# A chunked recurrence between dense products: two groups of small products per chunk and a third chunk in flight

## The chip, the cores and the metric

The kernel runs on one core of one Trainium2 chip. The time is the device time of one execution, in microseconds (us). The engines are PE (TensorE: matmuls, with its weight loads shown apart as PEld), DVE (VectorE), ACT (ScalarE), POOL (GpSimd) and SP (SyncE, which here only issues DMAs). Each engine works through its own list of instructions in order; semaphores hold an instruction back until what it needs is there.

## The reference, cut to what matters

The kernel computes one layer of a hybrid backbone for 1152 tokens (1024 latent, 128 context) of width 1024: a half-step feed-forward block, a mixer (latent attention beside a gated recurrence that runs in both directions over the tokens), and a second half-step feed-forward block. The change touches the recurrence alone. Per head (8 heads, key and value width 64) and direction, the reference is:

```
def hgrn2_chunked(q, k, logf, v, s0):
    ...
    b = jnp.cumsum(logf.reshape(B, n, CHUNK, H, DK), axis=2)
    diff = b[:, :, :, None] - b[:, :, None, :]
    decay = jnp.where(mask, jnp.exp(jnp.where(mask, diff, 0.0)), 0.0)
    A = jnp.einsum('bntshk,bnthk,bnshk->bnhts', decay, qc, kc)
    o_intra = jnp.einsum('bnhts,bnshv->bnthv', A, vc)
    dS = jnp.einsum('bnshk,bnshv->bnhkv', kc * jnp.exp(g[:, :, None] - b), vc)
    def step(S, inp):
        gj, dSj = inp
        return jnp.exp(gj)[..., None] * S + dSj, S
    ...
    o_inter = jnp.einsum('bnthk,bnhkv->bnthv', qc * jnp.exp(b), S_prev)
```

So for each block of tokens three things are wanted: the masked matrix A of decayed products of queries and keys, the state's increment dS, and the chain of states S, from which the outputs are A times V plus queries times S.

## The kernel before, in words

**Stages.** `run` does the first feed-forward block, then the mixer, then the second block. The mixer begins with `hgrn`, which holds both the recurrence and the large projections of the mixer's input. The projections are what keeps PE busy there: each is a dense product over 384 tokens, 24 matmuls (`mm3`, lines 551 to 553, written to a bank called `mm`), cut in two halves of 12. The recurrence consists of very small products, and they are put between halves of dense ones.

**Chunks.** The tokens are cut in three chunks of 384 (three blocks of 128), and the eight heads are taken one after another, so there are 24 chunks. Both directions of a head lie in the two halves of the 128 partitions. Per chunk:

- `scan_pre` (no matmuls) makes from the gates the scaled keys and queries of blocks of 8 tokens: Kb, Qb, and KE, QP, which carry the decay to the edge of the block. It is cut in five steps.
- `scan_lev` climbs the levels. Level 0 multiplies Kb with Qb in blocks (24 matmuls, two banks, one for each direction). The levels m = 8, 16, 32 and 64 each multiply a half-filled copy of the keys, `kr[m]`, with QP (12, 12, 12 and 6 matmuls, one bank). After a level's product DVE and POOL scale QP (line 1135), and DVE scales KE, by the decays of the neighbouring block; ACT makes the next `kr` from KE (`key_half`). So the product of a level needs QP as scaled after the level before it. Results are taken out of the banks by DVE under a mask (lines 1105, 1140) or by ACT (line 1124). Then KE is transposed (`kt`, line 1150), copied by ACT, and multiplied with V (`dS`, line 1160), which ACT copies out (line 1161).
- After the third chunk of a head, `scan_out` runs the chain of states on DVE (line 1170, 14 steps), multiplies A and S with V and QP (`po`, lines 1180 and 1183), and ACT copies the outputs. When four of these are done for a pair of heads, ACT squares the outputs (line 820), PE takes their means (`ops`, line 1194) and DVE and ACT normalise (`rstd`).

**Order.** A generator stands for each piece of work. For p = 0, 1, ... the loop in `hgrn` takes `cur` (the chunk p) and `old` (the chunk before) and alternates between `group(...)`, which takes one step of each generator named, and `slots(k)`, which takes k halves of dense products, with a step of `scan_pre` for the next chunk in each. There are three groups and 3, 2 or 3, and 2 slots per chunk. A scheduler then orders each engine's list by the order of the program and by when it expects operands, and it may move an instruction of DVE or ACT by some places.

**Banks.** Of the eight PSUM banks three are a ring for the levels (`lv`), two for the dense products (`mm`), and three for the rest (`sm`: kt, dS, po, the transposes of V called vt, and ops). A product that takes the next bank of a ring waits until what stood there has been read.

Of the kernel before, what the change touches and what calls it, by code (L numbers as in the profile page):

```python
# [9 lines left out]
F32 = mybir.dt.float32  # L10
# [9 lines left out]
P = 128  # L20
# [7 lines left out]
NCH = T // CW  # L28
# [5 lines left out]
H = 8  # L34
# [59 lines left out]
class Trunk:  # L94
# [783 lines left out]
    def hgrn(self):  # L878
# [76 lines left out]
            pass  # L955
        self.group()
        work = chain.from_iterable(map(work_of, range(H)))
        old = cur = out = last = None
        for p in range(H * NCH + 1):
            h, n = divmod(p, NCH)  # L960
            old, cur, pre = cur, None, iter(())
            if h < H:
                cur = self.scan_lev(d, ORDER[n])
            if p + 1 < H * NCH:
                h1, n1 = divmod(p + 1, NCH)
                while min(heads[h1].get("nf", 0), pairs[h1 // 2].get("nq", 0)) <= n1:
                    next(work)
                if n1 == 0:
                    last, d = d, scan_of(h1)
                pre = self.scan_pre(d, ORDER[n1])  # L970

            def slots(k):
                for _ in range(k):
                    next(work, None)
                    next(pre, None)
                    self.tick()

            self.group(old, cur)
            slots(3)
            self.group(old, cur, old, out)  # L980
            slots(2 + p % 2)
            self.group(cur, out, old)
            out = None
            if p and n == 0:
                out = self.scan_out(last if h < H else d)
                next(out)
            slots(2)
            for _ in pre:
                pass
        self.group(out, out)  # L990
        todo = list(range(KT // 2))
        for i, _ in enumerate(work):
            self.tick()
# [30 lines left out]
    def scan_pre(self, d, b):  # L1024
        nc = self.nc
        fs, q, QP, hh = d["f"], d["pair"]["q"], d["QP"], d["h"] % 2
        A, B = slice(0, 64), slice(64, P)
        c0 = b * CW
        X, Y = self.XY
        tmp = self.tmp  # L1030
        fv = fs[:, c0 : c0 + CW].rearrange("p (n e) -> p n e", e=8)
        kk = tmp("kk")
        nc.scalar.activation(kk[A], fs[A, c0 : c0 + CW], AF.Copy, scale=-1.0, bias=1.0)
        nc.scalar.activation(kk[B], fs[B, c0 + 1 : c0 + CW + 1], AF.Copy, scale=-1.0, bias=1.0)
        qx = tmp("qx")
        for r in (A, B):
            nc.scalar.copy(qx[r], q[64 * hh : 64 * hh + 64, c0 : c0 + CW])
        yield
        for out, pos, off, eng in ((X, (2, 1, 0), 1, nc.vector), (Y, (4, 5, 6, 7), 0, nc.gpsimd)):
            for n, o in enumerate(pos):  # L1040
                ov, iv = out[:, :, o : o + 1], fv[:, :, o + off : o + off + 1]
                if n == 0:
                    nc.scalar.copy(ov, iv)
                else:
                    eng.tensor_mul(ov, iv, out[:, :, pos[n - 1] : pos[n - 1] + 1])
        nc.vector.reciprocal(Y[:, :, 0:3], X[:, :, 0:3])
        yield
        nc.vector.reciprocal(X[:, :, 4:8], Y[:, :, 4:8])
        yield
        Kb, Qb, KE = tmp("Kb", 2), tmp("Qb", 2), tmp("KE", 3)  # L1050
        flat = lambda t: t.rearrange("p n e -> p (n e)")
        for r, x, y in ((A, X, Y), (B, Y, X)):
            nc.vector.tensor_mul(Kb[r], kk[r], flat(x)[r])
            nc.vector.tensor_mul(Qb[r], qx[r], flat(y)[r])
        yield
        TK, TQ, Tm = tmp("TK", 3, (P, 48)), tmp("TQ", 3, (P, 48)), tmp("T8", 3, (P, 48))
        f8 = fs[:, c0 + 8 : c0 + 8 + CW - 7 : 8]
        nc.vector.tensor_copy(TK[A], Y[A, :, 7])
        nc.vector.tensor_copy(TK[B], X[B, :, 0])
        nc.vector.tensor_mul(TQ[A], X[A, :, 0], fv[A, :, 0])  # L1060
        nc.vector.tensor_mul(TQ[B], Y[B, :, 7], f8[B])
        nc.vector.tensor_mul(Tm, TK, TQ)
        e8 = lambda t: t.rearrange("p (n e) -> p n e", e=8)
        bc = lambda t, m: t.unsqueeze(2).to_broadcast([t.shape[0], t.shape[1], m])
        qp = QP[:, c0 : c0 + CW]
        nc.vector.tensor_tensor(e8(KE), e8(Kb), bc(TK, 8), ALU.mult)
        nc.gpsimd.tensor_tensor(e8(qp), e8(Qb), bc(TQ, 8), ALU.mult)
        d["pre"] = Kb, Qb, KE, Tm
        yield

    def scan_lev(self, d, b):
        nc = self.nc
# [31 lines left out]
        for dst, mi, (_, ps) in zip((A1, A2), (0, 1), pair):  # L1104
            nc.vector.copy_predicated(dst, mb(mi), ps[:, :, :G])
        hm = lambda t, m: t.rearrange("p (n h m) -> p n h m", h=2, m=m)

        def key_half(m):
            kr = self.kr[m]
            nc.scalar.copy(hm(kr, m)[A, :, 0], hm(KE, m)[A, :, 0])  # L1110
            nc.scalar.copy(hm(kr, m)[B, :, 1], hm(KE, m)[B, :, 1])

        key_half(8)
        yield
        for li, m in enumerate((8, 16, 32, 64)):
            ps = lv()
            blocks = diag
            if m >= G:
                blocks = [(slice(u, u + m), slice(u + m, u + 2 * m)) for u in range(0, P, 2 * m)]
# [15 lines left out]
                eng.tensor_tensor(v, v, bc(tt[r], m), ALU.mult)  # L1135
            nc.vector.tensor_mul(Tn, tL, tR)
            if m < 64:
                key_half(2 * m)
            if m < G:
                nc.vector.copy_predicated(A1, mb(2 + li), ps[:, :, :G])  # L1140
            if m == 16:
# [1338 lines left out]
```

## Time and profile before

| | us |
|---|---|
| median of three runs | 2806.74 (2804.63 to 2808.57) |
| the profiled execution, its own time | 2808.74 |
| its span, first to last instruction | 2806.9 |
| PE busy, all of the span | 2755.8 (98%) |
| DVE busy, all of the span | 2044.2 (73%) |
| the recurrence: first level-0 product to last `ops` | 865 to 1388 |

The profile's rows give a start and a length in us, the engine, the line, the operation and the names as "written<-read", and in square brackets how long the engine stood idle before and what released it. A matmul's record is longer than the time until the next one starts, since they overlap: what counts on PE is the distance from start to start, some 0.17 to 0.18 us for a dense matmul here. A 32-wide or 64-wide product is shown as two records. The granted clock of PE was 1.00 of full speed all through the recurrence.

### The profile page before, as it was taken

How to read it: one execution, taken by the hardware profiler on the slowest of the kernel's cores; microseconds unless marked ns; L12 is line 12 of the kernel's file. 1: busy time of each engine (PE TensorE's matmuls, PEld its weight loads, DVE VectorE, ACT ScalarE, POOL GpSimd, SP SyncE). 2: the span in 40 equal slices, each digit the busy share in tenths (PEclk: the TensorE clock that was granted, in tenths of full speed). 3: DMA queues.
4: the chain of work that ended last, by engine and by line, in shares of the span. 5: the costliest groups of instructions: out<-in, count | busy, mean ns of one | idle time of the engine just before them, and what ended most of it. 6: DMA issues, size and time to landing. Idle time of an engine off the chain costs nothing. (4 is left out here: it accounts for less than half of the span.)

```text
span 2806.9 us, 55765 instructions
## 1 busy us (share of the span) xinstructions
PE 2755.8 (98%) x21248; PEld 2631.0 (94%) x21248; DVE 2044.2 (73%) x4461; ACT 1301.1 (46%) x2695; POOL 928.1 (33%) x983
## 2 busy tenths in 40 slices
PE   8999999999999999999999999999999999999998
PEld 8999999999999998899998788689999999999997
DVE  8877777677778888888456777867666765568875
ACT  6532323322166677666436777741642222334332
POOL 0133323454221222222233444431414343433451
PEclk9999999999999999999999999999999999999999
DMA  6733333653121111212512000273453444357521
GB/s 259 231 129 120 125 126 125 241 202 111 58 94 59 44 61 41 66 48 81 189 64 98 19 15 28 86 246 119 141 176 130 161 136 140 111 175 244 160 85 68
DMA packets 219579, 337.66 MB, mean 120 GB/s; under 512 B 23664, under 2 KB 141360, under 8 KB 219312
## 3 DMA queue, kind: packets, MB, share of 16 engines
q1 hardware_dynamic: 218880, 333.96, 35.5%
q8 instruction: 168, 2.75, 0.4%
q14 instruction: 99, 0.81, 0.1%
q10 hardware_dynamic: 432, 0.14, 0.0%
HBM read 248.47 MB, written 85.54 MB: 119 GB/s over the span
## 5 line engine op out<-in xcount | busy, mean ns | idle before, releaser
L1932 PE MATMUL b<-xo,wo 128*128 128x288 f32 x3552 | 483.7, 295 | 0.9 <-DVE wo L1907 0.9
L1932 PEld LDWEIGHTS b<-xo,wo 128*128 128x128 f32 x3552 | 475.4, 188 | 1.2 <-DVE wo L1907 1.2
L1932 PE MATMUL b<-bh,wo 128*128 128x288 f32 x1776 | 365.9, 295 | 0.0
L551 PE MATMUL mm<-xh,wh 128*128 128x384 f32 x928 | 322.9, 348 | 4.5 <-DVE sg L863 3.1
L553 PE MATMUL mm<-xh,wl 128*128 128x384 f32 x928 | 313.3, 338 | 0.0
L552 PE MATMUL mm<-xl,wh 128*128 128x384 f32 x928 | 312.5, 337 | 0.0
L1932 PEld LDWEIGHTS b<-bh,wo 128*128 128x128 f32 x1776 | 288.8, 188 | 0.0
L581 DVE SCALAR_TENSOR_TENSOR x<-dn,modt,x 128x256 f32<-128x256 f32 (+4 forms) x472 | 225.7, 499 | 82.3 <-PE dn L553 81.2
L1932 PE MATMUL b<-bl,wo 128*128 128x288 f32 x888 | 261.8, 295 | 0.0
L1906 ACT CAST wo<-raw 128x512 fp32r<-128x512 f32 x185 | 114.7, 621 | 222.5 <-issue 91.3
L2133 PE MATMUL d<-xd,wd 128*128 128x288 f32 x1344 | 181.5, 296 | 6.4 <-DVE x L2120 5.3
L2133 PEld LDWEIGHTS d<-xd,wd 128*128 128x128 f32 x1344 | 178.7, 188 | 9.1 <-issue 3.6
L1907 DVE TENSOR_TENSOR wo<-raw,wo 128x512 fp32r<-128x512 f32 x185 | 127.5, 690 | 80.4 <-ACT wo L1906 78.0
L551 PEld LDWEIGHTS mm<-xh,wh 128*128 128x128 f32 x928 | 174.2, 188 | 11.1 <-DVE sg L863 3.6
L552 PEld LDWEIGHTS mm<-xl,wh 128*128 128x128 f32 x928 | 174.4, 188 | 0.9
L553 PEld LDWEIGHTS mm<-xh,wl 128*128 128x128 f32 x928 | 174.5, 188 | 0.0
L1629 POOL TENSOR_TENSOR ehl<-e,ehl 128x512 fp32r<-128x512 f32 x93 | 124.1, 1339 | 151.3 <-ACT ehl L1627 80.4
L405 DVE SCALAR_TENSOR_TENSOR junk<-wada,cb 128x512 bf16<-128x512 f32 x224 | 164.7, 735 | 7.7 <-DMA wada<-in_w_aT 6.9
L1932 PEld LDWEIGHTS b<-bl,wo 128*128 128x128 f32 x888 | 167.4, 189 | 0.0
L1902 POOL TENSOR_TENSOR ws<-raw 128x256 f32<-128x256 f32 x74 | 69.8, 964 | 271.8 <-DMA raw<-in_w 242.9
L551 PE MATMUL ps<-bh,wh 128*128 128x288 f32 (+1 forms) x448 | 135.6, 303 | 1.4 <-DVE sl L1854 1.1
L1907 DVE TENSOR_TENSOR wo<-ws,wo 128x512 fp32r<-128x512 f32 x74 | 70.2, 948 | 86.4 <-ACT wo L1906 86.0
(478 smaller groups left out, 7172.5 us busy)
## 6 DMA issues: line engine op xcount, KB each, us to landing
raw<-in_w SPq DMA_DIRECT2D x148, 256.0 KB, 3.3
wada<-in_w_aT SPq DMA_DIRECT2D x112, 256.0 KB, 2.9
raw<-in_w SPq DMA_DIRECT2D x42, 512.0 KB, 3.9
raw<-in_w_in SPq DMA_DIRECT2D x41, 512.0 KB, 3.7
xr<-xd SPq DMA_DIRECT2D x56, 288.0 KB, 4.1
hr<-hs SPq DMA_DIRECT2D x26, 576.0 KB, 5.7
hb<-hd SPq DMA_DIRECT2D x44, 288.0 KB, 3.6
hs<-et SPq DMA_DIRECT2D x84, 144.0 KB, 2.2
```

The costliest lines, as they stand in the source:

```text
L405: nc.vector.scalar_tensor_tensor(junk, ws[n % 2], 1.0, cs[s], ALU.mult, ALU.mult, accum_out=o)
L551: pin(nc.tensor.matmul(ps, wh, xh, start=start and i == 0, stop=False))
L552: pin(nc.tensor.matmul(ps, wh, xl, start=False, stop=False))
L553: self.last_mm = nc.tensor.matmul(ps, wl, xh, start=False, stop=stop and i == n - 1)
L581: nc.vector.scalar_tensor_tensor(self.x[m][:, a:b], ps[:, a - lo : b - lo], self.modt[:, gm, m, s : s + 1], self.x[m][:, a:b], ALU.mult, A ...
L1629: eng.tensor_sub(el, e, eh)
L1902: nc.gpsimd.tensor_tensor(o[:, c], x[:, c], y[:, c], op)
L1906: nc.scalar.copy(wh, src[i])
L1907: nc.vector.tensor_sub(wl, src[i], wh)
L1932: nc.tensor.matmul(ps, w[:, k], x[:, k, :QW], start=first, stop=last, skip_group_check=home != i)
L2133: nc.tensor.matmul(ps, w[:, k], xv, start=start, stop=stop, skip_group_check=home != i)
```

## The change

The loop keeps three chunks in flight (`older`, `old`, `cur`) and has two groups per chunk, with 4 slots after the first and 3 or 4 after the second; it runs one round longer. Level 0 and the level of 8 are now one step of `scan_lev`; the `kr` for 8 is made at the end of `scan_pre`. The level of 8 takes its bank from the ring `sm` instead of `lv`. The chain of states begins after the first group of the second round of the next head, and both halves of the output products stand in the second group. No instruction is added or taken away on any engine.

```
-        old = cur = out = last = None
-        for p in range(H * NCH + 1):
+        older = old = cur = out = last = None
+        for p in range(H * NCH + 2):
             h, n = divmod(p, NCH)
-            old, cur, pre = cur, None, iter(())
+            older, old, cur, pre = old, cur, None, iter(())
...
-            self.group(old, cur)
-            slots(3)
-            self.group(old, cur, old, out)
-            slots(2 + p % 2)
-            self.group(cur, out, old)
+            self.group(older, old, cur)
             out = None
-            if p and n == 0:
+            if p > 1 and n == 1:
                 out = self.scan_out(last if h < H else d)
                 next(out)
-            slots(2)
+            slots(4)
+            self.group(out, old, cur, out, old)
+            slots(3 + p % 2)
             for _ in pre:
                 pass
-        self.group(out, out)
...
         nc.gpsimd.tensor_tensor(e8(qp), e8(Qb), bc(TQ, 8), ALU.mult)
+        self.key_half(KE, 8)
         d["pre"] = Kb, Qb, KE, Tm
         yield
+
+    def key_half(self, KE, m):
+        kr, src = [t.rearrange("p (n h m) -> p n h m", h=2, m=m) for t in (self.kr[m], KE)]
+        for r, side in ((slice(0, 64), 0), (slice(64, P), 1)):
+            self.nc.scalar.copy(kr[r, :, side], src[r, :, side])
...
-        key_half(8)
-        yield
         for li, m in enumerate((8, 16, 32, 64)):
-            ps = lv()
+            ps = self.pp.tile([P, 3, 64], F32, tag="sm", bufs=3, name="lv8") if m == 8 else lv()
...
             if m < 64:
-                key_half(2 * m)
+                self.key_half(KE, 2 * m)
```

How PE's list moves for one chunk, away from the ends of the recurrence. In these rows `kr_9121` is the `kr` of level 8, `kr_9122` of 16, `kr_9123` of 32 and `kr_9124` of 64, and "..." stands for halves of dense products (12 `mm` matmuls each). Before:

```order
L1098 MATMUL lv<-QP,kr_9123 32x32 x12
L1098 MATMUL lv<-Qb,Kb 32x32 x24
...
L1098 MATMUL lv<-QP,kr_9124 64x64 x6
L1098 MATMUL lv<-QP,kr_9121 32x32 x12
L1150 MATMUL kt<-ident,KE 128x128 x3
...
L1098 MATMUL lv<-QP,kr_9122 32x32 x12
L1160 MATMUL dS<-V,kT 64x64 x6
```

And now:

```order
L1155 MATMUL dS<-V,kT 64x64 x6
L1101 MATMUL lv<-QP,kr_9123 32x32 x12
L1101 MATMUL lv<-Qb,Kb 32x32 x24
L1101 MATMUL lv_10715<-QP,kr_9121 32x32 x12
...
L1101 MATMUL lv<-QP,kr_9124 64x64 x6
L1101 MATMUL lv<-QP,kr_9122 32x32 x12
L1145 MATMUL kt<-ident,KE 128x128 x3
```

The same 75 products of a chunk stand in two runs instead of three; dS is now that of the chunk two places back. Counted over the whole recurrence, from the first level-0 product to the last `ops`, PE's list has 77 runs of small products between dense ones before, and 54 in the change.

At the place where a pair's outputs are normalised (three times within the loop), PE's list before has

```order
L1098 MATMUL lv<-QP,kr_9122 32x32 x12
L1180 MATMUL po<-Af,V 64x128 x2
...
L1180 MATMUL po<-Af,V 64x128
L1160 MATMUL dS<-V,kT 64x64 x6
...
L1098 MATMUL lv<-QP,kr_9123 32x32 x12
L1098 MATMUL lv<-Qb,Kb 32x32 x24
L1194 MATMUL ops<-osq,onesb 128x384 x3
```

and now (`lv_11939` is the level of 8, in the ring `sm`)

```order
L1155 MATMUL dS<-V,kT 64x64 x6
L1101 MATMUL lv<-QP,kr_9123 32x32 x12
L1101 MATMUL lv<-Qb,Kb 32x32 x24
L1101 MATMUL lv_11939<-QP,kr_9121 32x32 x12
L1189 MATMUL ops<-osq,onesb 128x384 x3
```

Of the five tiles of the three-bank ring that this run fills, the second `ops` takes the bank of dS and the third takes that of the level of 8, both filled in the same run.

DVE's list after the first group, where a head's chain of states starts (the scaling of QP after level 32, the masked copies of level 0, the scaling after level 8, its masked copy, the chain, then KE for the next levels and the next chunk's Kb):

```order
L1130 TENSOR_TENSOR QP<-QP,T_10556 64x6x32
L1165 SCALAR_TENSOR_TENSOR S<-S,Gall,dS 64x64 x2
L1108 COPY_PREDICATED A_0_9127<-mask,lv 128x96
L1108 COPY_PREDICATED A_9129<-mask,lv 128x96
L1130 TENSOR_TENSOR QP<-QP,T_10600 64x24x8
L1135 COPY_PREDICATED A_0_9127<-mask,lv_10715 128x96
L1165 SCALAR_TENSOR_TENSOR S<-S,Gall,dS 64x64 x7
L1130 TENSOR_TENSOR KE<-KE,T_10875 64x6x32 x2
L1130 TENSOR_TENSOR KE<-KE,T_10923 64x24x8 x2
L1050 TENSOR_TENSOR Kb<-kk,X 64x384
```

The two scalings of QP stand next to their products; the chain follows at once. At the end of the recurrence PE's list had 24 dense matmuls between the last dS and the last outputs and 24 between these and the last `ops`; now it has 12 and 18.

More of the change, by code (lines that the diff above doesn't have):

```diff
@@ L1106, in scan_lev @@
         hm = lambda t, m: t.rearrange("p (n h m) -> p n h m", h=2, m=m)
[L1108 to L1111, printed above, removed]
-        key_half(8)
-        yield
         for li, m in enumerate((8, 16, 32, 64)):
-            ps = lv()
+            ps = self.pp.tile([P, 3, 64], F32, tag="sm", bufs=3, name="lv8") if m == 8 else lv()
             blocks = diag
```

## The prediction

> **What bounds the kernel now.** I read the page first, for the engine that is never free.
>
> ```profile
> PE 2755.8 (98%) x21248; PEld 2631.0 (94%) x21248; DVE 2044.2 (73%) x4461; ACT 1301.1 (46%) x2695; POOL 928.1 (33%) x983
> ```
>
> PE is, so whatever shortens PE's list or its waits in the recurrence shortens the kernel, as nothing else is near its limit over the span. Next the stretches: the recurrence whole, without its end, and its most crowded 80 us (columns: length, then busy time of PE, PEld, DVE, ACT, POOL, PE's clock, DMA).
>
> ```profile
> 865.00:1388.00 523.00, 511.26 (x6130) 477.86 (x6129) 405.59 (x1040) 348.31 (x862) 126.06 (x204) 1.00 0.22 73
> 865.00:1345.00 480.00, 468.26 (x5767) 437.58 (x5767) 391.90 (x1008) 327.29 (x821) 118.11 (x197) 1.00 0.18 60
> 1145.00:1225.00 80.00, 75.29 (x936) 69.77 (x935) 69.10 (x165) 53.62 (x133) 22.77 (x33) 1.00 0.16 50
> ```
>
> PE is idle for 523.0 - 511.3 = 11.7 us of the recurrence, at full clock. DVE is busy for 82% (391.9 of 480), in the worst stretch for 86%: not a bound, but an engine with a queue. Who PE waits for there (us in total, times, longest):
>
> ```profile
> PE lv L1098 <- DVE QP L1135: 7.0, 6, 1.8
> PE mm L551 <- DVE sg L863: 3.1, 2, 1.6
> PE lv L1098 <- DVE A L1105: 0.7, 1, 0.7
> PE lv L1098 <- POOL QP L1135: 0.3, 1, 0.3
> PE mm L551 <- DVE q L779: 0.3, 1, 0.3
> PE mm L551 <- ACT sg L751: 0.2, 1, 0.2
> ```
>
> So 8.0 us in 8 waits are level products that wait for the scaling of QP (or, once, for a bank); 3.6 us are dense products that wait for a bank of their own. Beside the waits there is a cost that counts as busy: the seam where PE goes from dense to small products and back. The timeline of PE around two runs, one of a level's product alone, one of dS alone:
>
> ```profile
> 1362.45 0.33 PE L552 MATMUL mm<-xl,wh 128*128 128x384 f32 x1
> 1362.62 0.34 PE L553 MATMUL mm<-xh,wl 128*128 128x384 f32 x1
> 1362.88 0.40 PE L1098 MATMUL lv<-QP,kr 128*32 128x32 f32 x24
> 1363.21 0.44 PE L551 MATMUL mm<-xh,wh 128*128 128x384 f32 x1
> 1363.49 0.34 PE L552 MATMUL mm<-xl,wh 128*128 128x384 f32 x1
> ...
> 1374.91 0.57 PE L1160 MATMUL dS<-V,kT 128*64 128x64 f32 x12
> 1375.41 0.44 PE L551 MATMUL mm<-xh,wh 128*128 128x384 f32 x1
> 1375.69 0.34 PE L552 MATMUL mm<-xl,wh 128*128 128x384 f32 x1
> ```
>
> Dense matmuls start 0.17 to 0.18 us apart (1362.45 to 1362.62). The last one before a run is followed after 0.26 us (1362.62 to 1362.88), the first one after it after 0.28 us (1363.21 to 1363.49, 1375.41 to 1375.69). The products themselves take 0.33 us (12 of a level) and 0.50 us (6 of dS).
>
> **The change part by part.** No instruction is added or removed; five things move.
>
> *Seams.* One costs 0.26 + 0.28 - 2 x 0.175 = 0.19 us. The lists have 77 runs before and 54 now: 23 x 0.19 = **-4.4 us**. Ends: by the two rows that I measured from, -4 to -5; that the products inside a run cost more when they are joined is bounded by the same seam at nought.
>
> [...]
>
> *Waits of the levels.* A level's product waits for DVE's scaling after the level before. How late DVE can be, in the worst case seen (PE's rows, then DVE's):
>
> ```profile
> 1161.45 0.89 PE L1098 MATMUL lv<-QP,kr 128*64 128x64 f32 x36
> ...
> 1168.85 0.40 PE L1098 MATMUL lv<-QP,kr 128*32 128x32 f32 x24 [1.82 <-DVE QP L1135]
> ```
>
> ```profile
> 1164.79 0.90 DVE L1196 SCALAR_TENSOR_TENSOR oT<-oT,vec,osq 128x384 f32<-128x384 f32 x1
> 1165.72 2.98 DVE L1135 TENSOR_TENSOR QP<-QP,T 64x192 f32<-64x192 f32 x2
> ```
>
> The products end at 1162.3, DVE comes to their QP only after the normalisation, and ends at 1168.7: 6.4 us, where PE gave it 1168.85 - 1.82 - 1162.3 = 4.7 us. Before, two or three halves of a dense product lie between a level and the next, 4.2 to 6.3 us (a half is 12 x 0.175 = 2.1 us). Now it is four halves after the first group and three or four after the second: 8.4 us, or at least 6.3 + 0.4 (kt) + 0.5 (dS) + 0.2 = 7.4 us. That is over 6.4.
>
> But DVE now has more to do in one interval. The rows of the normalisation:
>
> ```profile
> L456 DVE SCALAR_TENSOR_TENSOR rt<-ops,osq 128x384 f32<-128x384 f32 x9 | 4.8, 549 | 2.6 <-ACT osq L455 2.6
> L457 DVE SCALAR_TENSOR_TENSOR rt<-rt,osq 128x384 f32<-128x384 f32 x9 | 4.8, 550 | 0.0
> L458 DVE SCALAR_TENSOR_TENSOR osq<-rt,osq 128x384 f32<-128x384 f32 x9 | 5.3, 606 | 0.1
> L1196 DVE SCALAR_TENSOR_TENSOR oT<-oT,vec,osq 128x384 f32<-128x384 f32 x9 | 5.6, 640 | 0.0
> L1135 DVE TENSOR_TENSOR QP<-QP,T 64x192 f32<-64x192 f32 x96 | 39.4, 420 | 30.0 <-PE lv L1098 28.0
> ```
>
> A normalisation is 3 x (0.55 + 0.55 + 0.61 + 0.64) = 7.0 us. In an average interval of about 10 us DVE has 18% spare, 1.8 us, so it carries at most some 5.2 us into the next group. The list puts the two scalings right behind their products, so they wait for the carried work and their own 2 x 0.42 + three masked copies, some 1.7 us: 6.9 us, still under 7.4. The last row shows that DVE more often waits for PE (28.0 us) than PE for it. I leave 0.5 of the 8.0 us: **-7.5 us**. Ends: all 8.0 gone, or none.
>
> *Waits of the dense products.* Their two banks and their readers are the same. DVE comes to a gate's product up to 5.2 us late by the sum above, where a bank must be free after 4.2 us: 1.0 us at nine gate and ten query products is +19 if every one met it, but only two of them fell on such a place before. I take **0**; ends -2.5 and +6.
>
> *The ring of three banks.* Before, no run filled a bank of it twice. Now the third `ops` must wait for DVE's masked copy of the level of 8, the second for ACT's copy of dS. Rows for the length of `ops` (by form), and for the latest copy of a dS against its product (PE's row, then ACT's):
>
> ```profile
> L1194 PE MATMUL ops<-osq,onesb 128*128 128x384 f32 x24 | 8.7, 499 | 0.1
> ```
>
> ```profile
> 1061.97 0.57 PE L1160 MATMUL dS<-V,kT 128*64 128x64 f32 x12
> ...
> 1066.64 0.32 ACT L1161 COPY dS<-dS 128x192 f32<-128x192 f32 x1
> ```
>
> Four `ops` runs of three are 8.7 / 12 = 0.7 us each. After dS come 0.33 + 0.55 + 0.33 us of levels (level 0's 24 products take 0.55 us by the same start-to-start reading), then the first `ops`: the second is due 1.9 us after dS ends, the third 1.4 us after the level of 8. ACT's copy came up to 1066.96 - 1062.54 = 4.4 us after its product, so 2.5 us too late at worst; DVE, with 6.4 us as above, 5.3 us too late at worst, at best (0.42 + 0.27 us after the product) in time. One wait runs under the other, so a place costs 0 to 5.3 us, three places 0 to 16. Since the scheduler left the three `ops` together and DVE's list has the masked copy ahead of the chain and the next chunk's work, I take the low side: 0.3 us each, **+1 us**.
>
> [...]
>
> *The end.* The timeline of the last head, other engines (PE's dS row is above):
>
> ```profile
> 1375.76 0.31 ACT L1161 COPY dS<-dS 128x192 f32<-128x192 f32 x1
> 1375.88 1.29 DVE L358 TENSOR_TENSOR wl<-raw,wh 128x512 fp32r<-128x512 f32 x2 [3.05 <-ACT wh L354]
> 1377.21 2.79 DVE L1170 SCALAR_TENSOR_TENSOR S<-S,Gall,dS 64x64 f32<-64x64 f32 x9
> 1379.83 0.44 PE L1180 MATMUL po<-Af,V 128*64 128x128 f32 x4
> 1381.40 0.39 PE L1183 MATMUL po<-QP,S 128*64 128x128 f32 x4
> 1382.05 0.85 ACT L1186 COPY oT<-po 64x256 f32<-64x256 f32 x2 [0.34 <-PE po L1180]
> 1382.93 1.17 ACT L820 ACTIVATE osq<-oT 128x1152 f32<-128x1152 f32 x1
> ```
>
> The chain of states is done 1380.0 - 1374.9 = 5.1 us after dS begins. With 12 dense matmuls between, PE reaches the outputs 0.5 + 0.2 + 2.1 = 2.8 us after, and the last of them that needs a state 1.57 us later, at 4.4: 0.7 us of waiting. Then 18 dense matmuls (3.15 us) must cover copy and square (2.1 us from the last product's end) and a table load that the list puts between: nearly. Ends 0 and +3; I take **+1**. Within the loop the chain has 8.4 us and more, and needs 0.6 us for the copy and 14 x 0.32 = 4.5 us, so it hides.
>
> Sum: -4.4 - 7.5 + 0 + 1 + 1 = -9.9 us. Of the profiled execution's 2808.74 that leaves 2798.8; that execution is 2.0 us above the median of the runs, so against 2806.74 it is **2796.8 us**.
>
> **The rivals.** *The waits only move* (the seams go, the waits stay): DVE's work is the same, and at 86% busy in the worst stretch PE arriving sooner would only wait there for as long as it saved. For it: four of the waits stand between 1168 and 1192, behind one normalisation. Against: 86% is not 100%. Then -4.4 + 1 + 1 = -2.4: 2804.3.
>
> *The ring decides* (the slower side): three `ops` places and two where a transpose of V is the ring's next tile, each held 5.3 us, the worst above: 26.5 - 4.4 - 7.5 + 1 = +15.6: 2822. It decides against the change from (4.4 + 7.5 - 1) / 5 = 2.2 us per place. For it: copies were 4.4 us late at times; against: mostly they came within 0.6 us (1375.48 to 1376.07).
>
> *Seams are free when joined*, that is, what I count as a seam stays in another form inside the longer run: -7.5 + 1 + 1 = -5.5: 2801.2. [...]
>
> That fewer runs would not come about is excluded by the list.
>
> **How the numbers follow.** The forecast has 0.62, with its own range 2793 to 2801 (seams 4 to 5, level waits 6 to 8, dense waits and end at their ends); the waits that only move 0.24; free seams 0.08; the ring 0.06. A measurement of this kernel tells about 0.2% (5.6 us) from no change: faster is below 2801.1, slower above 2812.4. Faster: 0.58 + 0.04 + 0.02 = 0.64; slower: the ring and a little more, 0.07; within: 0.29. The range for 8 in 10 reaches from the forecast to the waits that only move: 2792 to 2805.
>
> **What would show it.** Right: in the list of waits the rows of QP (7.0 and 0.3) fall under 1.5 together; the 54 runs each still show 0.26 and 0.28 at their ends; `ops` waits under 1 us in all; the recurrence ends about 10 us sooner. Wrong: a row of `ops` or `vt` that waits for DVE or ACT by more than 2 us, dense products that wait for `sg` or `q` by more than 9 us, or runs whose products take longer than the parts did apart.

## The result, and the profile after

| | before | the change |
|---|---|---|
| median of four runs | 2807.56 us (2804.63 to 2808.57) | 2823.39 us (2821.79 to 2825.41) |
| the profiled execution, its own time | 2808.74 us | 2821.79 us |
| its span | 2806.9 us | 2820.0 us |

The change is slower: the ratio is 1.0054, with a 95% interval of 1.0042 to 1.0066, some 15 us. The forecast was 2796.8 us, with a range of 2792 to 2805.

The page's first part for the change, and the list of what PE waits for in the recurrence, which now ends at 1402:

```profile
PE 2760.8 (98%) x21248; PEld 2640.2 (94%) x21248; DVE 2045.4 (73%) x4461; ACT 1303.3 (46%) x2695; POOL 926.6 (33%) x983
```

```profile
PE mm L551 <- DVE sg L863: 8.0, 3, 4.0
PE mm L551 <- ACT sg L751: 6.7, 3, 2.8
PE po L1178 <- DVE S L1165: 2.7, 2, 2.0
PE mm L551 <- DVE q L779: 2.1, 2, 1.6
PE ops L1189 <- DVE A L1135: 0.7, 1, 0.7
PE vt L797 <- ACT dS L1156: 0.4, 1, 0.4
PE vt L797 <- ACT V L798: 0.3, 1, 0.3
```

The eight waits of level products (8.0 us) are gone, every one. In their place dense products wait for their own two banks: 16.8 us in eight waits, where it was 3.6 us in four. PE's waits are not fewer (13 in all, 12 before) but longer: the longest was 1.8 us, now it is 4.0. In all PE waits 20.9 us, 9.3 us more. DVE's work is the same (2045.4 us of the span, 2044.2 before).

The waits alone do not make the 13 us by which the spans differ. The table of stretches for the change, three of 20 us with a long stall in each (columns as before; PE's clock stands third from the end), and PE's timeline at one of the stalls:

```profile
1040.00:1060.00 20.00, 16.07 (x189) 14.55 (x188) 18.68 (x43) 8.96 (x25) 8.12 (x9) 0.93 0.23 73
...
1180.00:1200.00 20.00, 17.20 (x115) 16.61 (x114) 16.52 (x47) 12.46 (x30) 5.40 (x10) 0.83 0.19 55
...
1300.00:1320.00 20.00, 15.84 (x177) 14.76 (x176) 18.91 (x44) 8.69 (x24) 7.96 (x8) 0.91 0.22 70
```

```profile
1051.68 0.34 PE L552 MATMUL mm<-xl,wh 128*128 128x384 f32 x1
1051.87 0.34 PE L553 MATMUL mm<-xh,wl 128*128 128x384 f32 x1
1056.07 0.45 PE L551 MATMUL mm<-xh,wh 128*128 128x384 f32 x1 [3.87 <-DVE sg L863]
1056.36 0.34 PE L552 MATMUL mm<-xl,wh 128*128 128x384 f32 x1
...
1057.34 0.52 PE L551 MATMUL mm<-xh,wh 128*128 128x384 f32 x1
1057.66 0.52 PE L552 MATMUL mm<-xl,wh 128*128 128x384 f32 x1
1057.98 0.52 PE L553 MATMUL mm<-xh,wl 128*128 128x384 f32 x1
```

A microsecond after the stall the matmuls start 0.32 us apart, not 0.175: the granted clock is 0.50 from 1057.08 to 1060.49. Before, the clock was 1.00 all through. So the change's five stalls of 2.0 us and more are paid twice, as 0.50 was granted beside or behind each of them; after those of 1.6 and 1.8 us (1079.45 and 1153.63) the dense matmuls start 0.17 to 0.18 us apart.

The whole account is taken between the same two dense matmuls of PE's list, one ahead of the recurrence (855.68 before, 854.21 now) and the one behind its last `ops` (1389.23 and 1401.72), summed over all start times of PE between them:

| us | before | the change | difference |
|---|---|---|---|
| between the two matmuls | 533.6 | 547.5 | +13.9 |
| PE waits for something | 12.2 | 21.3 | +9.0 |
| dense matmuls over 0.175 us apart, the excess | 1.0 | 9.6 | +8.5 |
| the rest: the products themselves and their seams | 520.3 | 516.7 | -3.6 |

Of the excess in the change, 6.8 us are 47 matmuls that start 0.32 us after the one before; much of the rest falls on the first matmul or two behind a stall. The last line is what the change was to bring, and it is there. From one chunk's level 0 to the next chunk's, at the same place of PE's list (PE's rows, before and then the change):

```profile
1257.67 0.62 PE L1098 MATMUL lv<-Qb,Kb 64*32 64x32 f32 x48
...
1280.21 0.62 PE L1098 MATMUL lv<-Qb,Kb 64*32 64x32 f32 x48
```

```profile
1262.47 0.62 PE L1101 MATMUL lv<-Qb,Kb 64*32 64x32 f32 x48
...
1284.62 0.62 PE L1101 MATMUL lv<-Qb,Kb 64*32 64x32 f32 x48
```

22.54 us became 22.15 us in a chunk without a wait. Everything else is loss.

**The bank that comes late.** At the stall above, the readers of the product whose bank is wanted (ACT's sigmoid, then DVE's multiplication), and DVE's load in that gap, from one run of small products to the next:

```profile
1048.59 0.49 ACT L751 ACTIVATE sg<-mm 128x384 f32<-128x384 f32 x1
```

```profile
1055.46 0.56 DVE L863 TENSOR_TENSOR sg<-mm,sg 128x384 f32<-128x384 f32 x1
```

```profile
1043.60:1059.39 15.79, 11.86 (x157) 10.60 (x156) 15.27 (x35) 5.76 (x16) 6.74 (x7) 0.93 0.15 52
```

DVE is busy for 15.3 of 15.8 us and comes to the gate 6.4 us after the sigmoid's end (1049.08). The same place before, DVE and then PE:

```profile
1054.54 0.55 DVE L863 TENSOR_TENSOR sg<-mm,sg 128x384 f32<-128x384 f32 x1
```

```profile
1052.30 0.89 PE L1098 MATMUL lv<-QP,kr 128*64 128x64 f32 x36
1053.13 0.55 PE L1150 MATMUL kt<-ident,KE 128*128 128x128 f32 x3
1055.15 0.44 PE L551 MATMUL mm<-xh,wh 128*128 128x384 f32 x1 [1.47 <-DVE sg L863]
```

The bank came free at 1055.1 before, 0.9 us sooner. But PE had 1.4 us of small products to do ahead of the dense half that wanted it. They now stand behind that half.

The same can be read from the two timelines at every place inside the recurrence where the dense wait is over 1 us longer than before. Counted in us from the end of the product whose bank is wanted, first when its last reader is done, then when PE has nothing left to do ahead of the dense half that wants the bank:

| the half starts, in the change | reader done: before, the change | PE there: before, the change | wait: before, the change |
|---|---|---|---|
| 1056.07 | 6.9, 8.4 | 5.5, 4.6 | 1.5, 3.9 |
| 1079.45 | 7.0, 5.8 | 6.8, 4.2 | 0.3, 1.6 |
| 1153.63 | 0.5, 6.0 | 6.1, 4.2 | none, 1.8 |
| 1191.24 | 6.5, 8.3 | 6.3, 5.5 | 0.2, 2.8 |
| 1316.42 | 7.1, 8.6 | 5.5, 4.6 | 1.6, 4.0 |

So the reader was already late before, 6.5 us and more at four of the five, and two things came together: PE is there 0.8 to 2.6 us sooner at all five, and the reader is later still at four. The small products that stood between are gone at four places; at 1191 they are still there, and what is gone is a wait of a level product (0.7 us).

**The end.** PE, DVE's two slow steps of the chain of states, and POOL:

```profile
1389.61 0.44 PE L1175 MATMUL po<-Af,V 128*64 128x128 f32 x4
1390.83 0.44 PE L1178 MATMUL po<-QP,S 128*64 128x128 f32 x4 [0.78 <-DVE S L1165]
1391.07 0.42 PE L1175 MATMUL po<-Af,V 128*64 128x128 f32 x4
1393.45 0.44 PE L1178 MATMUL po<-QP,S 128*64 128x128 f32 x4 [1.97 <-DVE S L1165]
```

```profile
1387.77 2.29 DVE L1165 SCALAR_TENSOR_TENSOR S<-S,Gall,dS 64x64 f32<-64x64 f32 x1 [4.04 <-ACT dS L1156]
...
1390.72 2.37 DVE L1165 SCALAR_TENSOR_TENSOR S<-S,Gall,dS 64x64 f32<-64x64 f32 x1
```

```profile
1387.58 2.40 POOL L366 TENSOR_TENSOR wl<-raw,wh 128x1024 fp32r<-128x1024 f32 x1 [6.60 <-ACT wh L365]
1390.66 2.34 POOL L366 TENSOR_TENSOR wl<-raw,wh 128x1024 fp32r<-128x1024 f32 x1 [0.69 <-ACT wh L365]
```

A step that took 0.28 us each of nine times before (2.79 us for nine, one after the other) took 2.29 and 2.37 us where POOL was splitting a weight of the next stage; both ended within 0.1 us of POOL's instruction. Before, POOL's first such split began at 1380.19, when the chain was done.

### The profile page after: what moved, and what is told of

The parts are those of the page before. It is cut to its first block, busy times and chain, and to the rows that moved or that the text cites. A ratio compares the mean times of both kernels' runs of the same rounds, so it can differ in the third digit from the quotient of the medians.

```text
span 2820.0 us, 55704 instructions
## 1 busy us (share of the span) xinstructions
PE 2760.8 (98%) x21248; PEld 2640.2 (94%) x21248; DVE 2045.4 (73%) x4461; ACT 1303.3 (46%) x2695; POOL 926.6 (33%) x983
```

## The experiments

The theory from this profile: DVE, and ACT which waits for DVE in its own order, are late beside a normalisation in both kernels. With two groups PE meets this lateness in few long stalls at the dense banks; one of 2.0 us or more costs clock too (0.50 granted at all five of them); and the end is a loss of its own, POOL's. The rivals: the ring of three banks (`sm`, called the small ring below); the moved copies of the level of 8, which hold up ACT; the way DVE's work is divided between the two gaps or ordered in its list.

| kernel | median, us | ratio to the kernel before | 95% interval |
|---|---|---|---|
| the change | 2823.4 | 1.0054 | 1.0042 to 1.0066 |
| lv8_back | 2830.6 | 1.0082 | 1.0065 to 1.0099 |
| parts_three_groups | 2806.2 | 0.9995 | 0.9986 to 1.0005 |
| no_newton | 2806.6 | 0.9997 | 0.9987 to 1.0006 |
| before_no_newton | 2801.5 | 0.9975 | 0.9966 to 0.9984 |
| split_on_dve | 2816.1 | 1.0032 | 1.0019 to 1.0045 |
| no_newton_split | 2802.8 | 0.9979 | 0.9969 to 0.9988 |
| first_chunk_and_split | 2816.1 | 1.0027 | 1.0017 to 1.0036 |
| slots_five_two | 2822.6 | 1.0048 | 1.0031 to 1.0065 |
| gate_ahead_dve | 2824.4 | 1.0052 | 1.0037 to 1.0067 |
| third_dense_bank | 2816.9 | 1.0031 | 1.0019 to 1.0043 |
| third_bank_split | 2813.6 | 1.0015 | 1.0006 to 1.0023 |
| third_bank_before | 2808.0 | 0.9997 | 0.9989 to 1.0006 |
| prep_behind_kt | 2835.8 | 1.0095 | 1.0081 to 1.0109 |
| prep_behind_kt_split | 2831.8 | 1.0077 | 1.0061 to 1.0092 |
| third_bank_kt | 2828.3 | 1.0066 | 1.0053 to 1.0078 |
| third_bank_kt_first_chunk | 2825.7 | 1.0056 | 1.0043 to 1.0069 |
| spread_norm_split | 2813.4 | 1.0020 | 1.0011 to 1.0029 |
| spread_norm_before | 2807.6 | 0.9997 | 0.9988 to 1.0005 |

**Which part of the change.** Undo the bank, or make only the two smaller parts of the change, the bank and the copies for the level of 8:

```
  lv8_back: the change with
-            ps = self.pp.tile([P, 3, 64], F32, tag="sm", bufs=3, name="lv8") if m == 8 else lv()
+            ps = lv()

  parts_three_groups: the kernel before with
-        key_half(8)
         yield
...
-            ps = lv()
+            ps = self.pp.tile([P, 3, 64], F32, tag="sm", bufs=3, name="lv8") if m == 8 else lv()
...
+        self.key_half(KE, 8)
```

(the last line at the end of `scan_pre`).

> The change, but the bank of the level of 8 comes from the levels' ring again, as before. If late readers of the dense banks cost the time (my theory), this stays at 2821 to 2824 us: only the waits on the small ring (0.7 us of ops, 0.4 and 0.3 us of vt) can go, and the stalls of 2 to 4 us before dense products stay. If the ring of three banks is the cause, it falls below 2813 us and the dense products stop waiting.

> The kernel before with its three groups, but with the other two parts of the change: the copies for the level of 8 at the end of the chunk's preparation, and that level's bank from the small ring. If the joining of the groups costs the time, this runs as the kernel before, 2806 to 2810 us, with the waits of level products (7 us or so) still there. If the moved copies hold up ACT, sigmoids behind them come late here too, and it takes 2814 us or more.

lv8_back came out at neither: 7 us slower than the change. Its list of PE's waits begins

```profile
PE lv L1101 <- ACT Af L1119: 8.8, 17, 3.2
PE lv L1101 <- DVE A L1108: 7.2, 3, 5.8
PE mm L551 <- DVE sg L863: 7.2, 3, 3.2
```

The level of 32, level 0 with its two banks and the level of 8 want four banks in one run, of a ring of three, and PE waits 16.0 us for that ring. So the move to the other ring is no loss but what the joining needs; that part of the prediction (+1 us) holds. parts_three_groups is the kernel before within 0.1%, with its 6.9 us of waits for QP. So neither of these two parts alone is the cause. What is left is the new loop: two groups, a third chunk in flight, and the chain and the outputs at another place.

**Is it DVE's load?** Leave out the Newton step of the output normalisation (it refines the reciprocal square root), in the change and, as control, in the kernel before:

```
-        self.rstd(sq[:, cs], ps, pin=lambda i: self.roots.append(self.behind(i, table)))
+        self.roots += [self.behind(nc.scalar.activation(sq[:, cs], i, f, **k), table) for i, f, k in
+            ((ps, AF.Ln, dict(bias=self.epst)), (sq[:, cs], AF.Exp, dict(scale=-0.5)))]
```

> The change, but the output normalisation leaves out its Newton step (three DVE instructions of 0.55 to 0.61 us for each of three column blocks, 5.1 us of DVE work per pair of heads). If DVE's backlog in the gap behind a normalisation makes the dense products wait, the stalls of 3.9 us (at 1056), 2.8 us (at 1191) and 4.0 us (at 1316) fall under 1 us each and PE's clock stays full there: 10 us of waiting and some 5 us of slow matmuls less, 2807 to 2811 us. If the order of ACT's list alone (the copies for the level of 8, moved ahead) or the ring is the cause, the stalls stay and the time is over 2819 us.

> The kernel before, with the Newton step of the output normalisation left out (5.1 us of DVE work per pair of heads), as the control to the change without it (2806.6 us, 16.8 us less than with it). If only the joined groups make PE stand on DVE's load there, this gains no more than its short waits behind a normalisation: 2802 to 2807 us. If it gains as much as the change did (12 us or more), the load is a price that both pay and does not explain the difference.

Without these 5.1 us per pair of heads (20.4 us over the recurrence, 15.3 of them within the loop) the change gains 16.8 us by the medians (by the ratios 0.57%, 16 us), the kernel before 7.0 us (0.25%). Both pay for the load, the change more than twice as much. PE's waits for the gates' multiplication, in the change without the step and in the kernel before without it:

```profile
PE mm L551 <- DVE sg L863: 0.6, 2, 0.4
```

```profile
PE lv L1098 <- DVE QP L1135: 4.4, 4, 1.4
PE mm L551 <- DVE sg L863: 2.2, 3, 1.0
```

The stalls at 1056, 1191 and 1316 fell to 0.2, 0.4 and 0.4 us. The other waits of dense products stay: 2.1 us at the start and 1.7 us at 1148 for ACT's sigmoid, and for q 2.4 us (1.6 before the step was left out) with another of 1.0 us. These are not shown to be the normalisation's. The end is worse: the last outputs wait 5.2 us, since both of POOL's splits now fall on the chain (its nine steps take 6.74 us beside them, not 2.79). That the load costs the kernel before 7 us too was more than I had expected (2802 to 2807 us; it is 2801.5).

**The end.** The two weight splits from POOL to DVE, alone and without the Newton step:

```
-        ws = [self.load_w(self.a["w_in"][i0 + i], KT, P) for i in range(n)]
+        ws = [self.load_w(self.a["w_in"][i0 + i], KT, P, home="low" if n == 2 else None) for i in range(n)]
```

> The change, but the two weight splits that POOL does beside the last chain of states (2.40 and 2.34 us) are done by DVE in two halves each. If POOL's reads hold DVE up, the two steps of the chain that took 2.29 and 2.37 us take 0.28 us, the last outputs wait under 0.8 us instead of 2.75 us, the clock stays full there, and the kernel takes 2817 to 2820 us. If the end is too short for the chain in any case (12 dense matmuls ahead of the outputs), the wait stays over 2 us and the time at 2822 us or more.

> The change without the Newton step (left out as before) and with the weight splits beside the last chain of states on DVE. The load beside a normalisation and the blocked chain at the end are the two large losses by my account, and they stand apart: 2799 to 2803 us. If the stall of 5.2 us before the last outputs (seen without the Newton step) is not POOL's doing, it stays, and the time is 2805 us or more.

DVE's row of the same nine steps in split_on_dve:

```profile
1389.43 2.79 DVE L1165 SCALAR_TENSOR_TENSOR S<-S,Gall,dS 64x64 f32<-64x64 f32 x9
```

The steps are back at 0.31 us from start to start, although DVE now does the splits as well (1.29 us each); the outputs wait 1.2 us, not 2.7, and the kernel is 7.3 us faster than the change by the medians (0.22%, 6.2 us, by the ratios), 1 us more than expected. no_newton_split is within its expectation, 2802.8 us: load and blocked chain together are worth 20 us, more than the change had lost. But the kernel before without the step is at 2801.5 us: with both losses away the two groups are still no gain.

**Is it how the work is divided or ordered?** Five halves after the first group and two or three after the second; the gate's reader ahead of the next chunk's keys in DVE's list; the preparation of the next chunk behind the copy of the transposed KE in ACT's list (`behind` sets an order on one engine, not a wait):

```
  slots_five_two
-            slots(4)
+            slots(5)
...
-            slots(3 + p % 2)
+            slots(2 + p % 2)

  gate_ahead_dve
-            nc.vector.tensor_mul(Kb[r], kk[r], flat(x)[r])
+            self.behind(nc.vector.tensor_mul(Kb[r], kk[r], flat(x)[r]), *self.gates)

  prep_behind_kt
-        nc.scalar.activation(kk[A], fs[A, c0 : c0 + CW], AF.Copy, scale=-1.0, bias=1.0)
+        self.behind(nc.scalar.activation(kk[A], fs[A, c0 : c0 + CW], AF.Copy, scale=-1.0, bias=1.0), *self.kts)
```

Here `gates` holds the last multiplication of line 863, and `kts` the last copy of kt; the copies of kk[B] and qx are treated like kk[A].

> The change, but five halves of dense products after the first group and two or three after the second, not four and three or four. If the division of DVE's work between the two gaps is at fault (15.3 us of it came in the gap after the first group at 1043.6, 7.3 us in the one before), the longer gap takes up to 2.1 us from each of the stalls of 3.9 and 4.0 us, these stay below 2 us, PE's clock stays full there, and the time is 2814 to 2818 us. If DVE's load over the whole stretch is what counts, the stalls stay or turn into waits of level products for QP (3 us and more), and the time is 2822 us or more.

> The change, but on DVE the scaling of the keys for a coming chunk is put behind the multiplication that reads a gate's product out of its dense bank (an order, not a wait). If the order of DVE's list alone is at fault, the dense products' waits for that multiplication (8.0 us) fall under 2 us, nothing takes their place, and the time is 2808 to 2814 us. If DVE has too much to do in the stretch, what is put back comes late instead: level products wait for Qb, Kb or QP by 4 us or more in all, and the time stays within 5 us of the change's 2823.

> The change with one order on ACT: the copies with which a chunk's preparation begins (kk, qx) stand behind the last copy of a transposed KE, so that the preparation, and with it four to six us of DVE's work per chunk, begins after the second group and not ahead of it. If what comes too late is DVE's and ACT's work bunched in one gap by their lists, the stalls of 2.8 to 4.0 us before dense products fall under 2 us and the time is 2808 to 2816 us. If DVE's load over a whole chunk beside a normalisation is what counts, however it is divided, the stalls stay within 1 us of what they were, or products of levels wait for Kb, Qb or QP, and the time is 2820 us or more.

> The same order, with the weight splits beside the last chain of states on DVE. The two stand apart, so by either reading it is 6 to 8 us less than with the order alone: 2801 to 2809 us if bunching is at fault, 2812 us or more if the load is.

None of them helps. slots_five_two has stalls of 3.9, 3.7 and 4.0 us at the same places and 3.7 us at `ops` beside them. In gate_ahead_dve the dense products wait 17.5 us, as before (its rival, waits of level products, did not come either). prep_behind_kt is the worst of all, and its list of PE's waits says why:

```profile
PE ops L1189 <- DVE A L1135: 12.8, 3, 4.7
PE mm L551 <- DVE sg L863: 8.0, 2, 4.0
```

With the preparation later, the masked copies that free the small ring for `ops` come up to 4.7 us late, on top of the old stalls. With the splits moved as well it is 2831.8 us, 4 us less, where 6 to 8 were expected. My reading that the scheduler's early preparation bunches DVE's work was wrong: begun later, it costs 12 us more.

**A third bank for the dense products.** If the dense banks are where the lateness is met, give them one more (PE's list stays as it is):

```
-        self.mmb = 2
-        for tag, n in (("lv", 3), ("mm", 2), ("sm", 3)):
+        self.mmb = 3
+        for tag, n in (("lv", 2), ("mm", 3), ("sm", 3)):
...
-            ps = self.pp.tile([P, 3, 64], F32, tag="sm", bufs=3, name="lv8") if m == 8 else lv()
+            ps = self.pp.tile([P, 3, 64], F32, tag="sm", bufs=3, name="lv8") if m in (8, 32) else lv()
```

> The change with a third bank for the dense products: the levels' ring has two banks, and the level of 32 takes its bank from the small ring, as the level of 8 does. PE's list is the same. If late readers of the two dense banks cost the time, a bank is wanted 4.2 us later than now: the dense products' waits (16.8 us) fall under 4 us, the half clock behind them goes, and the time is 2804 to 2812 us. If DVE's lateness then shows at the next product that needs it, level products wait for QP by 5 us or more again, or ops for its ring by 5 us or more, and the time is over 2814 us.

> As with the third dense bank, and the weight splits beside the last chain of states on DVE, which alone took 7.3 us off the change. If the two losses stand apart, the gains add up: 2797 to 2805 us, faster than the kernel before. If the end is late for another reason once PE comes there sooner, the outputs wait for the states by 2 us or more and it takes 2806 us or more.

> The kernel before (three groups) with the same three dense banks: the level of 32 in the small ring, two banks for the other levels. If joining the groups pays once the dense banks allow for it, this gains no more than its own dense waits of 3.6 us: 2802 to 2808 us, with 7 to 8 us of waits for QP left. If the bank alone is the gain, it is as fast as the change with the third bank and the splits moved, 2805 us or less by as much.

The dense products do not wait at all any more, but third_dense_bank misses its expectation by 5 us. PE's waits in it:

```profile
PE dS L1155 <- ACT kT L1147: 9.6, 2, 6.3
PE po L1178 <- DVE S L1165: 3.5, 3, 2.0
PE vt L797 <- ACT V L798: 3.4, 1, 3.4
```

The lateness shows at the next product that needs it: dS waits 6.3 and 3.3 us for ACT's copy of kt, which stands in ACT's list behind copies (qx, kk) that wait for DVE. It is half of the second reading that was on record, with another product than it named. With the splits moved too, 2813.6 us: 10 us less than the change, where 18 or more were expected of the two together. The kernel before gains nothing measurable from the bank (0.9997).

Two more on the third bank, with the order of prep_behind_kt, the second also with the first chunk's copies for the level of 8 behind the sigmoids ahead of the loop:

> The change with the third dense bank and the moved splits (2813.6 us), and the same order on ACT. Its stalls of 6.3 and 3.3 us were dS waiting for ACT's copy of KE, which stood behind kk and qx, and these waited for DVE. If an in-order wait of ACT for DVE is what remains, both stalls go with the half clock behind them (12 us in all), and the time is 2799 to 2806 us. If DVE's lateness only shows at yet another product, waits of over 8 us in all stand elsewhere and the time is 2809 us or more.

> As the last one, with the copies for the level of 8 of the first chunk behind the sigmoids of the products before the loop, so that ACT does not stand still for DVE at the start of the recurrence. If the 3.4 us stall of a transposed V at 867 follows from that, it goes and the time is 3 to 5 us less than without; if not, it is the same within 2 us.

As above, the later preparation loses more than it gives: `ops` waits 10.0 us for the masked copies, and the stalls of dS (2.5 us left of 9.6) are paid for there. The stall of `vt` at the start goes from 3.3 to 1.0 us with the first chunk's copies, and the time falls 2.6 us, somewhat less than expected. Without the third bank the same edit did not pay:

```
-            self.nc.scalar.copy(kr[r, :, side], src[r, :, side])
+            self.behind(self.nc.scalar.copy(kr[r, :, side], src[r, :, side]), *(self.sigs[-1:] if self.cnt < 1 else []))
```

> The change with two edits: the weight splits beside the last chain of states on DVE instead of POOL (alone 2816.1 us), and ACT's copies for the level of 8 of the very first chunk put behind the sigmoids of the products before the loop. If the stall of 2.1 us at 861 is ACT waiting in order for DVE's scaled keys with a sigmoid behind it, the stall and the 1.8 us of half clock after it go, and the time is 2811 to 2813.5 us. If something else holds that bank, it stays at 2815 us or more; if the level of 8 then waits for its copies, a wait of a level product of 1 to 2 us appears at 867 and half the gain is lost.

The stall at 861 went, but the median is that of split_on_dve. In split_on_dve's profile that stall had not cost any clock (1.00 from 858 to 867), so only its 2.1 us were to be had, and a new wait of 0.7 us for a sigmoid came at 899; the wait of a transposed V (1.0 us) stayed. Why none of the rest shows in the median is open.

**Spread the load.** Nothing left out, the normalisation's last three steps for one column block per group:

```
-            for b in ORDER:
-                self.rec_norm(b, oT, sq, table)
+            ends = [self.rec_norm(b, oT, sq, table) for b in ORDER]
+
+            def step(k):
+                ends[k]()
+                if k < 2:
+                    self.later.append(partial(step, k + 1))
```

`rec_norm` does the first step and gives back a function for the other three, the first of them behind the last masked copy; what is appended to `later` is done in the next group. (Not shown: `rt` gets a third buffer, and the last pair two more groups behind the loop.)

> The change with the moved splits (2816.1 us), nothing left out, and the normalisation's DVE work divided: the first step for all three column blocks at once, the other three steps (1.8 us) for one block per group, each behind a masked copy of that group. If DVE's load in one gap is what makes the banks late, the stalls of 3.9, 4.0 and 2.8 us fall under 2 us with the half clock behind them, and the time is 2802 to 2809 us. If the load over the two or three gaps counts, it stays at 2812 us or more.

> The kernel before with the same division of the normalisation (over three of its groups). Its waits for QP behind a normalisation are 1 to 1.8 us each; if they are the load of one gap too, 3 to 5 us go: 2803 to 2806 us. If the division only moves them, 2807 to 2810 us.

2813.4 us, against 2816.1 without the spreading: the stalls of 3.9 and 4.0 us fell to 2.3 and 2.4 and that of 2.8 went, but a wait for q rose from 1.6 to 3.5 us, and a new one of 2.2 us came at 1203. That profile's own time is 2818.6 us, 5 us above the median, so it tells where the waits stand and not how large the gain is. It fits the second reading: the load over several gaps counts, not that of one.

No kernel with nothing left out beat the kernel before; parts_three_groups, third_bank_before and spread_norm_before can't be told from it.

## Why the prediction was wrong

- **Seams** (-4.4): right. -3.6 us, which still holds some small products at half clock. The rival that joined seams stay in another form falls.
- **Waits of the levels** (-7.5 of 8.0): right, all 8.0 went.
- **Waits of the dense products** (0; ends -2.5 and +6): this is the step that failed. They rose by 13.2 us. I had the right place and a price of 1.0 us for each that is met (5.2 us late against 4.2), and then took none because "only two of them fell on such a place before"; the list of waits above that sentence has four. At these same four places the waits rose from 3.6 to 12.3 us, 3 us each, and four new ones made 4.6 us. The price was mis-sized: from the product's end (1047.7) to the free bank (1056.0) are 8.4 us, since ACT's sigmoid ended 1.4 us after the product, DVE came 6.4 us after that, and the multiplication itself holds the bank for 0.56 us; PE came back after 4.5. And neither the number of places nor their price carries over from an order in which PE came to the bank later (the table above). The sum also left out the chain through ACT (at 1191 the sigmoid, behind `kk`, which had waited 5.0 us for DVE).
- **The ring of three banks** (+1): right, 1.4 us (0.7 at `ops`, 0.4 and 0.3 at two `vt`).
- **The end** (+1; ends 0 and +3): mis-sized, +2.7 of waiting and about 1 of slow matmuls. The chain was costed at 0.32 us a step; two steps took over seven times that, beside POOL. The prediction moved the chain to a later time and did not ask what POOL does then.
- **The clock**: not in the sum at all. The slow dense matmuls add 8.5 us, most of it half clock. The forecast took a stall to cost its length.
- **The rivals**: "the waits only move" had the mechanism, but too small: it let PE wait no longer than before (11.6 us), and PE waits 20.9. That the waits get longer than those they replace, and that long ones cost clock, was in no case. The ring did not decide: its 2822 us lies next to the measured 2823.4 by luck, since it was to cost 26.5 us and cost 1.4. The stated sign of error, dense products that wait for `sg` or `q` by more than 9 us, is what the profile shows (10.1 us, 16.8 with ACT's sigmoid).
- **The range**: by the ends of its own terms (seams -5 and -4, levels -8 and -6, dense waits -2.5 and +6, ring +1, end 0 and +3) the sum runs from -14.5 to 0, which is 2792 to 2807 us. The stated 2793 to 2801 left out the upper end of the very term that failed.

That DVE's load beside the normalisations is what the three longest dense waits hang on, and that POOL blocked the chain, is shown by taking each away. Together they account for the loss: without both, the change is within 0.1% of the kernel before without the step, their intervals overlapping. No run moved the splits in the kernel before; that they cost nothing there is read from its timeline, where POOL's first began behind the chain. Why two groups are still no gain with both losses away (2802.8 against 2801.5 us) stays open: that profile has 4.4 us more of waits and 3.5 us more of slow matmuls than its control, at the start, at a wait for q (2.4 us) and at the last outputs (1.9 us), against 3.3 us of seams saved. But its own time is 2807.0 us, 4.2 above its kernel's median, so it shows more than the 1.4 us between the medians.

## What to carry to other kernels

A change that leaves the bottleneck engine fewer, longer stretches takes no work from the engines that feed it: cost their lateness from the end of the producing instruction to the free buffer, through every in-order engine between, at the new place of the consumer, and not by how often it was met before. Several short waits can be cheaper than the same time in long stalls: here the kernel before had twelve waits of up to 1.8 us at a granted clock of 1.00, and the change's five stalls of 2.0 to 4.0 us each went with 3.4 or 6.8 us at 0.50. Where a serial chain on DVE is moved in time, look at what POOL does at the new place: two steps beside it took 2.29 and 2.37 us here, and 0.28 us without it.

## What the runs showed of the hardware

- **Stalls and the clock.** Counted over the profiles of all twenty kernels here, from 840 to 1420 us: of 73 stalls of PE of 0.8 to 1.5 us one was followed by dense matmuls 0.32 us apart, of 26 from 1.5 to 2.0 us eleven, of 21 from 2.0 to 2.5 us fourteen, and of 42 longer ones all (one of them by the granted clock, 0.50, since small products followed it). The half clock lasted for 3 to 17 dense matmuls, and cost 0.4 to 2.5 us, most often about 1.4. The same stall of 2.1 us at the start cost it in five profiles and not in four.

The granted clock in the change's profile: in this stretch it is 0.50 five times, from 862.52, 1057.08, 1316.49 and 1395.00 for 3.41 us each and from 1190.20 for 6.83 us, and these starts are whole multiples of 3.413 us apart. In the 3.41 us ahead of each PE was idle for 2.02, 2.41, 3.35, 1.87 and 1.75 us. Of the other stretches of that length, counted on from the same starts, the one with most idle time had 1.63 us, and the clock stayed at 1.00 behind it. In the kernel before, no 3.41 us between 840 and 1420 held more than 1.82 us, and the clock was 1.00. Two stretches of that length around the stall of 2.1 us at the start, in the change and then in split_on_dve (columns as before):

```profile
859.10:862.52 3.42, 1.40 (x8) 1.40 (x9) 2.76 (x10) 2.14 (x5) 0.87 (x1) 1.00 0.16 57
862.52:865.93 3.41, 3.41 (x13) 3.41 (x12) 1.29 (x2) 3.30 (x7) 0.00 (x0) 0.50 0.29 67
```

```profile
856.25:859.66 3.41, 1.70 (x10) 1.38 (x8) 3.25 (x10) 0.41 (x2) 1.22 (x1) 1.00 0.00 0
859.66:863.08 3.42, 3.04 (x17) 3.05 (x18) 2.47 (x8) 3.31 (x7) 0.00 (x0) 1.00 0.16 58
```

In the change PE was idle for 2.0 us in the first, and the second ran at half clock; in split_on_dve the two hold 1.7 us and 0.4 of the same stall, and the clock stayed at 1.00. That it matters how a stall lies to these stretches is my estimate from the two pairs of rows and the starts above; no run tests it.

- **DVE beside POOL.** In the recurrence of the kernel before, 91 of DVE's instructions took at least 0.1 us longer than the same instruction usually does (its lower quartile), 36 us in all, and every one of them overlapped one of POOL's, though POOL is busy for only 126 of the 523 us (237 of DVE's 1040 instructions overlapped one of POOL's at all). The two steps of 2.29 and 2.37 us in the change ended 0.08 us after POOL's instructions of 2.40 and 2.34 us, and moving POOL's work away (split_on_dve) brought the nine steps back to 2.79 us in all.
